# Four Strassen blocks per FFN, one more weight sum made by transfers, and sums ahead of splits

## The chip, the cores and the metric

The kernel runs on one core of one Trainium2 chip. The metric is device time in microseconds; three runs of the kernel before gave 925.48, 925.88 and 926.36, median 925.88.

## What is computed

A trunk of two encoder layers on 256 tokens of width 1024, all in float32. Each layer is FFN, mixer, FFN, each closed by a residual and a layer norm; the mixer is a bidirectional mLSTM in layer 0 and windowed attention in layer 1. The change touches the four FFNs alone:

```
def swiglu(x, w_in, w_out):                  # x: (256, 1024)
    gu = x @ w_in                            # w_in: (1024, 5632)
    g, u = gu[..., :D_FF], gu[..., D_FF:]    # D_FF = 2816
    return (jax.nn.silu(g) * u) @ w_out      # w_out: (2816, 1024)

x = layer_norm(ALPHA * x + 0.5 * swiglu(x, ...), g, b)
```

## The kernel before

**Split products.** A float32 matrix product is made of three TensorE matmuls: each operand is split into a high part (`_hi`, rounded to the matmul's type) and a low part (`_lo`, the remainder), and `mm3` adds hi·hi, hi·lo and lo·hi in PSUM. Activations are split once. Every weight piece, 128 partitions by 1024 values (512 KB), is loaded into a raw buffer, ScalarE (ACT) writes `w_hi` (`Weights.high`, L214) and VectorE (DVE) writes `w_lo` as raw minus hi (`Weights.low`, L238).

**An FFN before.** The 2816 gate columns and the same number of up columns are worked off as: 512 columns wide, plain; then three groups (`GROUPS`), each a 256-column unit (plain: 48 matmuls of 512 columns, weight pieces that hold 256 gate beside 256 up columns) and a 512-column block in Strassen's form (`seven`): the two token tiles, the two halves of the 1024 rows, and gate beside up make a 2x2 by 2x2 block product that takes seven products of 12 matmuls instead of eight. Between them stand the `w_out` chunks (`down`, 12 matmuls each into four banks `py`): 16 of an FFN's 22 chunks are spread over groups and blocks, the last six make the tail.

**The block.** Its weights are eight raw pieces in four quarters (two pieces each): b11, b12 and b22, held in the `s_raw` buffers, and the fourth one "a", loaded plainly through `w_raw`. Sums of quarters are made in place: b11 is split (s1), then DVE adds b12 to it, it is split again (s5), DVE adds b22, it is split again (s6), and the fourth quarter is added to it by an accumulating DMA that GpSimd (POOL) issues (L267). After s6 DVE also adds b22 to b12. Then b12, b22 and b11 are split. So a block has 14 splits, 6 sums on DVE and 2 accumulating DMAs; TensorE's seven products use the parts in the same order, and the sums of the activations (`S1` to `S4`) are made once per FFN. DVE and ACT also combine the products (tiles `e1`, `e2`, `e5`, `g1`), and TensorE turns the result for `w_out` (`tr`): token tile 0 at the block's end, token tile 1 in the next stretch of work; ACT and DVE write its `h_hi` and `h_lo`.

**What orders the work.** Splits and sums are recorded by a planner in the program, not by a hand-written order. `Paced` keeps a rough clock for each engine; after every TensorE instruction `Weights.fill` (L270) records further highs, lows and sums as long as ACT's and DVE's planned clocks are no more than 300 ns ahead of TensorE's, the raw data are due, and at most `RING` = 10 split pieces stand ahead of the ones in use. Within `fill` a low goes before a sum. What is recorded is a fixed order on each engine, and each engine works its order off one by one. Loads are issued by SyncE (SP) right after the low or sum that frees a buffer: four `w_raw` buffers, two more (`v_raw`) for the FFN's own pieces, and six `s_raw` buffers used in turn.

**The tail.** After the last block the planner is off: `take_rows(6)` (L884) records the splits of the last six chunks as far as they are still missing, `W.done(0)` records as many of the next stage's first splits as the ring has room for (four), and only then `tail` (L569) records the last products: six chunks for token tile 0 (two halves `o` of the columns), `norm[0].half` and the rest of its layer norm on DVE, and the same for token tile 1, with the turn of the last block's token tile 1 (`between`) after ten of token tile 0's twelve chunk products, and `emit_x` (the normalized tile is turned into `xT` for the next stage) near the end.

Of the kernel before, what the change touches and what calls it, by code (L numbers as in the profile page):

```python
# [16 lines left out]
D = 1024  # L17
# [6 lines left out]
GROUPS = 3  # L24
RAW_BUFS = 4
S_RAW = 6
# [120 lines left out]
class Weights:  # L147
# [5 lines left out]
    def __init__(self, nc, pool, words, plan, after):  # L153
        self.nc, self.pool, self.words, self.plan, self.after = nc, pool, words, plan, after
        self.raw, self.parts, self.half, self.sums = {}, {}, [], []
        self.made = self.used = self.room = 0
        self.todo = {tag: [i for i, w in enumerate(words) if w["tag"] == tag] for tag in ("w_raw", "s_raw")}
        self.free = {"w_raw": RAW_BUFS, "v_raw": 0, "s_raw": 0}
# [14 lines left out]

    def open(self, pool, end, s_raw=S_RAW, v_raw=V_RAW):

        self.spool, self.send, self.vbufs = pool, end, v_raw
        self.free["s_raw"], self.free["v_raw"] = s_raw, v_raw
        self.load()

    def load(self, most=None):  # L180
# [3 lines left out]
        while most is None or n < most:  # L184
# [10 lines left out]
            pool, bufs = {"w_raw": (self.pool, RAW_BUFS), "v_raw": (self.spool, self.vbufs), "s_raw": (self.spool, S_RAW)}[in_]  # L195
# [74 lines left out]
    def fill(self):  # L270

        nc = self.nc
        while True:
# [7 lines left out]
            if vec < nc.pe + AHEAD:  # L281
                if self.half and nc.when(self.half[0][1]) < vec + SOON:
                    self.low()
                    continue
                if self.sums and nc.when(*(self.raw[w] for w in self.sums[0][1:] if isinstance(w, int))) < vec + SOON:
                    self.sum()
                    continue
            break

    def take(self, n):  # L290
        i = self.used
        self.used += n
        self.split(self.used)
        return [self.parts[j] for j in range(i, i + n)]
# [4 lines left out]
    def done(self, upto=None, most=None, high_only=False):  # L299
# [3 lines left out]
        for j in [j for j in self.parts if j < upto]:  # L303
            del self.parts[j]
        self.room = max(self.room, upto + RING)
# [15 lines left out]
def trunk_kernel(ctx: ExitStack, tc: tile.TileContext, x, ffn_w_in, ffn_w_out, ln_g, ln_b, ml_w_in, ml_gate_b,  # L321
# [17 lines left out]
    def split_of(w, scale=None, needs=None):  # L339

        plan.append(dict(word=w, k=words[w]["k"], scale=scale, needs=needs))
        return len(plan) - 1
# [97 lines left out]
    W = Weights(nc, wpool, words, plan, after)  # L440
# [173 lines left out]
    def ffn(l, i, n, pending, last):  # L614
        with ExitStack() as ph:
# [170 lines left out]
            def seven(full, unit_turn):  # L786
# [36 lines left out]
                unit_turn()  # L823
# [16 lines left out]
            turn = None  # L840
            for g in range(GROUPS):
                ps = [wbank(), wbank()]
                pieces = []
                for a in range(4):
                    pieces.extend(W.take(1))
                    for t in range(2):
                        for k in (2 * a, 2 * a + 1):
                            mm3(ps[t], pair(xT, A, k, tok(t)), pair(pieces[a], A, k % 2), k == 0, k == 7)
                    W.done()
                    if g == 0 and not start:  # L850
                        for n_, f_ in zip(XP[1:], (x_three, x_two, x_four)):
                            if a == n_:
                                f_()
                    if a == 1:
                        if g:
                            turn()
                        else:
                            for t in range(0 if start else 1, 2):
                                tr(hB0, t, hs[t])
                hh = []  # L860
                for t in range(2):
                    sg = temp("sg")[:, 0:256]
                    nc.scalar.activation(sg, ps[t][:, 0:256], AF.Silu)
                    hh.append(temp("hh")[:, 0:256])
                    nc.vector.tensor_mul(hh[t], sg, ps[t][:, 256:512])
                hp = h_room(2)
                chunks(hp, 2)
                down(1)

                def unit_turn(hp=hp, hh=hh):  # L870
                    p = wbank((128, 2, S))
                    for t in range(2):
                        for k in range(2):
                            nc.tensor.transpose(p[:, k, tok(t)], hh[t][:, k * 128:(k + 1) * 128], ident)
                    split_evac(hp, p)

                down(1)
# [557 lines left out]
```

## Time and profile before

| | |
|---|---|
| median of three runs | 925.88 us |
| span of the profiled execution | 924.3 us |
| around the span (median less span) | 1.6 us |
| busy: TensorE, DVE, ACT, POOL | 914.6, 785.0, 544.8, 107.0 us |
| mean granted TensorE clock | 0.998 |
| one group (256-column unit and block), on TensorE | 47.7 us |

How to read the views: in the chain and the timeline a line is start, duration, engine, what, and in brackets the idle time just before it and who ended it. In the windows a line is the stretch, its length, then busy time and instruction count of PE (TensorE), PEld (weight loads), DVE, ACT and POOL, the granted clock, the DMA engines' busy share and GB/s. In the groups a line is line, engine, operation, output<-inputs, shapes and count, then busy time and mean ns of one.

### The profile page before, as it was taken

What the parts mean: (1) busy time and instruction counts of PE and PEld (TensorE: products, weight loads), DVE (VectorE), ACT (ScalarE), POOL (GpSimd) and SP (SyncE); (2) the same over time, 40 slices, a digit from 0 to 9 for tenths busy, and PEclk for the clock granted to TensorE, in tenths of its full rate; (3) what the DMA queues carried; (4) which work ended last, traced back from release to release, by engine and by line L of the source; (5) the groups of instructions that cost most, each with busy time, mean ns of one, the idle gap of its engine ahead of it and who ended that gap; (6) DMA issues with size and microseconds to landing.
All of it is one profiled execution on the core that took longest, in us unless ns stands there. A gap on an engine that the chain in (4) does not pass through costs nothing.

```text
span 924.3 us, 12533 instructions
## 1 busy us (share of the span) xinstructions
PE 914.6 (99%) x4507; PEld 767.0 (83%) x4507; DVE 785.0 (85%) x949; ACT 544.8 (59%) x765; POOL 107.0 (12%) x154
## 2 busy tenths in 40 slices
PE   9999999999999999999999999999999999999996
PEld 7788888889988888888888888888888888888885
DVE  5899997886799799988887898988869878998876
ACT  5656756446664548565636566565569555757460
POOL 0010103013211010101010101010435300110100
PEclk9999999999999999999999999999999999999999
DMA  8969773655635949685558697737434385969431
GB/s 276 361 166 333 203 277 73 227 160 177 212 103 171 343 117 341 169 305 137 160 172 328 151 327 210 262 76 228 148 127 137 94 272 204 276 194 343 124 88 45
DMA packets 98525, 187.55 MB, mean 203 GB/s; under 512 B 6776, under 2 KB 37520, under 8 KB 98464
## 3 DMA queue, kind: packets, MB, share of 16 engines
q1 hardware_dynamic: 91072, 173.04, 54.9%
q0 software_dynamic: 6816, 12.67, 8.6%
q10 hardware_dynamic: 576, 1.05, 0.3%
q8 instruction: 35, 0.57, 0.2%
q14 instruction: 26, 0.21, 0.1%
HBM read 185.68 MB, written 1.05 MB: 202 GB/s over the span
## 4 chain that ended last, share of the span: by engine, by line
PE 93%; DVE 3%; ACT 1%; DMA 1%; issue 1%; POOL 0%; SPq 0%; DVEq 0%; POOLq 0%; ACTq 0%
PE pw L138 60%; PE py L138 33%; DVE w_lo L138 1%; ACT w_hi L138 1%; DVE h L138 1%; DMA w_raw<-in_ffn_w_out_dram 1%; DMA w_raw<-in_ffn_w_in_dram 0%; POOL hrs L1072 0%; DVE wt L138 0%; DVE x L138 0%; DVE hst L138 0%; SPq L102 0%; ACT xT_hi L138 0%; DVE stats L138 0%; ACT sg L138 0%
## 5 line engine op out<-in xcount | busy, mean ns | idle before, releaser
L138 DVE TENSOR_TENSOR w_lo<-w_raw,w_hi 128x1024 fp32r<-128x1024 f32 (+1 forms) x237 | 281.6, 1219 | 24.7 <-ACT w_hi L138 21.6
L138 ACT CAST w_hi<-w_raw 128x1024 fp32r<-128x1024 f32 (+1 forms) x237 | 241.2, 1049 | 82.1 <-PE py L138 27.3
L138 PE MATMUL pw<-w_hi,xT_hi 128*128 128x512 f32 x560 | 221.6, 397 | 0.0
L138 PE MATMUL pw<-w_lo,xT_hi 128*128 128x512 f32 x560 | 217.6, 390 | 0.5 <-DVE w_lo L138 0.5
L138 PE MATMUL pw<-w_hi,xT_lo 128*128 128x512 f32 x560 | 218.0, 391 | 0.0
L138 ACT CAST w_hi<-s_raw 128x1024 fp32r<-128x1024 f32 x144 | 148.1, 1052 | 78.5 <-DVE s_raw L138 42.1
L138 DVE TENSOR_TENSOR w_lo<-s_raw,w_hi 128x1024 fp32r<-128x1024 f32 x144 | 172.9, 1220 | 21.6 <-ACT w_hi L138 21.0
L138 PE MATMUL py<-w_hi,h_hi 128*128 128x512 f32 x349 | 136.9, 392 | 0.0
L138 PE MATMUL py<-w_hi,h_lo 128*128 128x512 f32 x349 | 136.0, 390 | 0.0
L138 PE MATMUL py<-w_lo,h_hi 128*128 128x512 f32 x349 | 135.9, 390 | 0.0
L138 PEld LDWEIGHTS pw<-w_hi,xT_lo 128*128 128x128 f32 x560 | 105.0, 188 | 22.5
L138 PEld LDWEIGHTS pw<-w_lo,xT_hi 128*128 128x128 f32 x560 | 105.3, 188 | 22.0 <-DVE w_lo L138 1.6
L138 PEld LDWEIGHTS pw<-w_hi,xT_hi 128*128 128x128 f32 x560 | 105.1, 188 | 20.0
L267 POOL DMA_DIRECT2D s_raw<-in_ffn_w_in_dram x24 | 29.2, 1217 | 511.6 <-DVE w_lo L138 429.0
L138 DVE TENSOR_TENSOR s_raw<-s_raw 128x1024 f32<-128x1024 f32 x72 | 87.2, 1221 | 1.0
L138 PEld LDWEIGHTS py<-w_hi,h_lo 128*128 128x128 f32 x349 | 65.5, 188 | 13.8
L138 PEld LDWEIGHTS py<-w_lo,h_hi 128*128 128x128 f32 x349 | 65.6, 188 | 13.6 <-DVE w_lo L138 0.3
L138 PEld LDWEIGHTS py<-w_hi,h_hi 128*128 128x128 f32 x349 | 65.5, 188 | 13.2
L138 PE MATMUL pw<-w_hi,S_hi 128*128 128x512 f32 x192 | 74.7, 389 | 0.0
L138 PE MATMUL pw<-w_lo,S_hi 128*128 128x512 f32 x192 | 74.7, 389 | 0.0
L138 PE MATMUL pw<-w_hi,S_lo 128*128 128x512 f32 x192 | 74.7, 389 | 0.0
L138 DVE TENSOR_TENSOR h_lo<-pw,h_hi 128x512 fp32r<-128x512 f32 x44 | 30.2, 688 | 26.5 <-ACT h_hi L138 26.5
(205 smaller groups left out, 1102.3 us busy)
## 6 DMA issues: line engine op xcount, KB each, us to landing
w_raw<-in_ffn_w_out_dram SPq DMA_DIRECT2D x88, 512.0 KB, 5.3
s_raw<-in_ffn_w_in_dram SPq DMA_DIRECT2D x72, 512.0 KB, 6.0
w_raw<-in_ffn_w_in_dram SPq DMA_DIRECT2D x56, 512.0 KB, 4.8
w_raw<-in_ffn_w_in_dram SPq DMA_DIRECT2D x96, 256.0 KB, 3.9
s_raw<-in_ffn_w_in_dram POOLq DMA_DIRECT2D x24, 512.0 KB, 6.0
w_raw<-in_ml_w_in_dram SPq DMA_DIRECT2D x24, 512.0 KB, 4.7
w_raw<-in_at_w_in_dram SPq DMA_DIRECT2D x12, 512.0 KB, 4.9
w_raw<-in_ml_w_out_dram SPq DMA_DIRECT2D x8, 512.0 KB, 4.1
```

The costliest lines, as they stand in the source:

```text
L138: r = f(out, *args, **kw)
L267: nc.gpsimd.dma_start(t.rearrange("p (k f) -> p k f", k=self.words[w]["k"]), v, accum_op=OP.add)
```

## The change

- Three groups become one 256-column unit (with its two `down` chunks) and four blocks in a row, each with four `down` chunks but the last, which has two. The unit's loop body is now straight code.
- In a block one more sum goes to DMA: after s1 and its DVE sum, an accumulating DMA adds to b12 the same weights that b22 holds (rows 512 and up of the up columns, read once more from memory), instead of DVE adding b22 to it after s6. A block then has 14 splits, 4 sums on DVE and 4 accumulating DMAs.
- `fill` now records a due sum before a low.
- The order of splits and the order of use part: chunks `down(1)` and `down(3)` are split ahead of the pieces that wait for sums, and used after them (`turn` += 2.5); the ring counts from the oldest piece not yet used.
- The six `s_raw` buffers become three tags of two (`s_raw0` to `s_raw2`), rotated from block to block so that the next b11 takes the buffers of the b12 before it.
- The layer norm's gain and bias rows take the tag `s_raw1`.

```
-GROUPS = 3
+SEVENS = 4
-S_RAW = 6
+S_RAW = 2
+TAGS = ("w_raw", "s_raw0", "s_raw1", "s_raw2")
...
             if vec < nc.pe + AHEAD:
+                if self.sums and nc.when(*(self.raw[w] for w in self.sums[0][1:] if isinstance(w, int))) < vec + SOON:
+                    self.sum()
+                    continue
                 if self.half and nc.when(self.half[0][1]) < vec + SOON:
                     self.low()
                     continue
-                if self.sums and nc.when(*(self.raw[w] for w in self.sums[0][1:] if isinstance(w, int))) < vec + SOON:
-                    self.sum()
-                    continue
...
     def take(self, n):
-        i = self.used
+        these = self.order[self.used:self.used + n]
         self.used += n
-        self.split(self.used)
-        return [self.parts[j] for j in range(i, i + n)]
+        self.split(max(these) + 1)
+        return [self.parts[j] for j in these]
...
-        self.room = max(self.room, upto + RING)
+        while self.gone < upto:
+            j = self.order[self.gone]
+            self.left.discard(j)
+            self.parts.pop(j, None)
+            self.gone += 1
+        self.room = max(self.room, min(self.left, default=len(self.plan)) + RING)
...
-    def seven(w, c0, c1, downs):
+    def seven(w, c0, c1, n, downs):
...
-        b12, b11, b22 = ([word(x, 2, "s_raw") for x in at(*p)] for p in ((0, c1), (0, c0), (512, c1)))
+        b12, b11, b22 = ([word(x, 2, TAGS[1 + (r + n) % 3]) for x in at(*p)]
+                         for r, p in ((1, (0, c1)), (0, (0, c0)), (2, (512, c1))))
         s1 = [split_of(w_) for w_ in b11]
         for a in at(512, c0):
             piece(a, 2)
-        for j in range(2):
-            after[s1[j]] = [(b11[j], b12[j])]
+        for j, a in enumerate(at(512, c1)):
+            after[s1[j]] = [(b11[j], b12[j]), (b12[j], a)]
         downs(0)
         s5 = [split_of(w_, None, p) for w_, p in zip(b11, s1)]
+        downs(1)
         for j in range(2):
             after[s5[j]] = [(b11[j], b22[j])]
         s6 = [split_of(w_, None, p) for w_, p in zip(b11, s5)]
         for j, a in enumerate(at(512, c0)):
-            after[s6[j]] = [(b11[j], a), (b12[j], b22[j])]
-        downs(1)
-        [split_of(w_, None, p) for w_, p in zip(b12, s6)]
+            after[s6[j]] = [(b11[j], a)]
+        plan[s6[0] - 1]["turn"] += 2.5
+        [split_of(w_, None, p) for w_, p in zip(b12, s1)]
         for w_ in b22:
             split_of(w_)
         downs(2)
+        downs(3)
         [split_of(w_, None, p) for w_, p in zip(b11, s6)]
-        downs(3)
+        if n < SEVENS - 1:
+            plan[-3]["turn"] += 2.5
...
-            for g in range(GROUPS):
-                c0 = 512 + 768 * g
-                for a in range(4):
-                    beside(wi, a * 256, c0, F + c0)
-                down(2)
-                seven(wi, c0 + 256, F + c0 + 256, lambda i_: down(1) if g < GROUPS - 1 or i_ < 2 else None)
+            for a in range(4):
+                beside(wi, a * 256, 512, F + 512)
+            down(2)
+            for g in range(SEVENS):
+                c0 = 768 + 512 * g
+                seven(wi, c0, F + c0, g, lambda i_: down(1) if g < SEVENS - 1 or i_ < 2 else None)
             down(6)
...
-            gb = load_ln(lambda name: pool.tile([128, D], F32, name=name, tag="s_raw", bufs=S_RAW), l, n)
+            gb = load_ln(lambda name: pool.tile([128, D], F32, name=name, tag=TAGS[1 + SEVENS % 3], bufs=S_RAW), l, n)
```

More of the change, by code (lines that the diff above doesn't have):

```diff
@@ L784, in copied, with seven @@
                 return e
-            def seven(full, unit_turn):
+            def seven(full, before):
                 of = lambda k0, t: (lambda k: pair(xT, A, k0 + k, tok(t)))
@@ L838, in seven @@
                 return lambda: tr(hB, 1, v["u1"])
[L840 to L860, printed above, removed]
-                for t in range(2):
[L862 to L877, printed above, removed]
-                turn = seven(g < GROUPS - 1, unit_turn)
-                if start and g == GROUPS - 1:
-                    small_loads()
@@ new lines, in ffn @@
+            ps = [wbank(), wbank()]
+            pieces = []
+            for a in range(4):
+                pieces.extend(W.take(1))
+                for t in range(2):
+                    for k in (2 * a, 2 * a + 1):
+                        mm3(ps[t], pair(xT, A, k, tok(t)), pair(pieces[a], A, k % 2), k == 0, k == 7)
+                W.done()
+                if not start:
+                    for n_, f_ in zip(XP[1:], (x_three, x_two, x_four)):
+                        if a == n_:
+                            f_()
+                if a == 1:
+                    for t in range(0 if start else 1, 2):
+                        tr(hB0, t, hs[t])
@@ new lines, in ffn, with turn @@
+            hh = []
+            for t in range(2):
+                sg = temp("sg")[:, 0:256]
+                nc.scalar.activation(sg, ps[t][:, 0:256], AF.Silu)
+                hh.append(temp("hh")[:, 0:256])
+                nc.vector.tensor_mul(hh[t], sg, ps[t][:, 256:512])
+            hp = h_room(2)
+            chunks(hp, 2)
+            down(1)
+            def turn():
+                p = wbank((128, 2, S))
+                for t in range(2):
+                    for k in range(2):
+                        nc.tensor.transpose(p[:, k, tok(t)], hh[t][:, k * 128:(k + 1) * 128], ident)
+                split_evac(hp, p)
```

29 lines of the change are left out of this document (18 added, 11 removed).

## The prediction

> **What bounds the kernel now.** I read the page's head and chain first, then the chain in order of time (start, duration, what), the window of one group (its length, then busy time of PE, PEld, DVE, ACT, POOL, granted clock, DMA share, GB/s), and last the timeline of each engine around an FFN's tail.
>
> ```profile
> span 924.3 us, 12533 instructions
> PE 914.6 (99%) x4507; PEld 767.0 (83%) x4507; DVE 785.0 (85%) x949; ACT 544.8 (59%) x765; POOL 107.0 (12%) x154
> PE 93%; DVE 3%; ACT 1%; DMA 1%; issue 1%; POOL 0%; SPq 0%; DVEq 0%; POOLq 0%; ACTq 0%
> ...
> 62.74 2.97 PE py L138 x12
> ...
> 377.15 5.44 PE py L138 x24
> 382.59 5.93 PE pw L138 x28
> ...
> 365.80:413.50 47.70, 47.70 (x218) 39.49 (x217) 44.32 (x44) 30.82 (x36) 2.39 (x2) 1.00 0.80 257
> ```
>
> TensorE is busy for 99% of the span and is 93% of the chain that ends last. 24 matmuls take 5.44 us: one each 0.2267 us (a record lasts longer, since they overlap); 28 with four transposes take 5.93, so four transposes cost 0.49. A group (204 matmuls, 12 transposes) is 46.2 + 1.5 = 47.7 us, just what its window is: TensorE never waits in it, with DVE busy for 44.3 of it. So matmuls saved are time saved, as long as DVE, DMA and the order of work keep up.
>
> **Part 1: fewer matmuls.** Two 256-column units (48 matmuls each) go, one block (84) comes: 12 fewer per FFN, 48 in all; in the built order the PE instructions fall from 4509 to 4461, transposes unchanged. 48 x 0.2267 = **-10.9 us**, all on the path.
>
> **Part 2: DVE's and ACT's work.** The built order has 24 more splits, 8 fewer DVE sums and more small products' work.
>
> ```profile
> L138 DVE TENSOR_TENSOR w_lo<-s_raw,w_hi 128x1024 fp32r<-128x1024 f32 x144 | 172.9, 1220 | 21.6 <-ACT w_hi L138 21.0
> ...
> 454.14 2.35 DVE L138 TENSOR_TENSOR w_lo<-w_raw,w_hi 128x1024 fp32r<-128x1024 f32 x2
> 456.41 0.68 DVE L138 TENSOR_TENSOR h_lo<-pw,h_hi 128x512 fp32r<-128x512 f32 x1
> 457.01 0.68 DVE L138 TENSOR_TENSOR e<-g,e 128x512 f32<-128x512 f32 x1
> 457.61 2.51 DVE L138 TENSOR_TENSOR w_lo<-w_raw,w_hi 128x1024 fp32r<-128x1024 f32 x2
> ```
>
> One low lasts 1.22, two end after 2.35, so the pitch is 1.14; for 128x512 it is 0.60 (456.41 to 457.01). A block with four `down` chunks takes TensorE 132 x 0.2267 + 8 transposes (0.98) = 30.9 us. DVE's part was 24 x 1.14 + 7 x 0.60 = 31.6 and becomes 22 x 1.14 + 4.2 = 29.3. Before, a block ran over by 0.7 and the unit behind it gave that back; now blocks follow each other with 1.6 us to spare each, and the last one (TensorE 25.5, two chunks fewer; DVE 27.0) runs over by 1.5. I cost the blocks at nothing: the cover is this 1.6 plus the lead of the splits. The built order shows that lead, counted in TensorE time from an evacuation to the first use of the next piece not yet split: some 9 to 21 us in the blocks of before from the second on, now 4 to 13 in every block. In the first block of an FFN it was already down to 7.0 before (5.7 and 2.95 in the first FFN), and the only wait there is the 2.97 at 62.74, 0.25 over 12 x 0.2267. In that place the lead is now 7.5: **-0.25**.
>
> **Part 3: transfers.** Rows of the DMA issues and queues, of two windows, and of one issue by itself:
>
> ```profile
> s_raw<-in_ffn_w_in_dram POOLq DMA_DIRECT2D x24, 512.0 KB, 6.0
> q0 software_dynamic: 6816, 12.67, 8.6%
> 386.00:388.00 2.00, 2.00 (x10) 1.60 (x10) 1.27 (x2) 2.00 (x3) 0.00 (x0) 1.00 1.13 197
> 396.00:398.00 2.00, 2.00 (x11) 1.65 (x10) 1.93 (x2) 1.71 (x4) 0.00 (x0) 1.00 1.05 392
> s_raw<-in_ffn_w_in_dram POOLq DMA_DIRECT2D x1, 512.0 KB, 7.5
> ```
>
> 24 accumulating transfers become 64. While two of them run (386 to 388) the DMA engines move 197 GB/s, without them 392; their share of the span, 8.6% of 924.3 over 24, is 3.3 us each, against 0.524/0.392 = 1.34 for a load. A block then needs 12 x 1.34 + 4 x 3.3 = 29.3 of its 30.9 us: 95%. The urgent ones are the two into b11. By the built order the second is issued behind the second s6 low, 7.8 us into the block (6.0 where DVE takes the second product, + 0.6 + 1.14), and b11's low stands ahead of DVE's reading of the fifth product, which ends at 19.5 (seven stretches of 2.72 and four transposes); less 1.05 for the high and 1.22 for the low, 9.5 us may pass. The trace has 6.0 as the median and 7.5 as the slowest (the last row, the second of a pair). So nothing is charged, with little room. By the Trainium skill, "DMA: Bandwidth & Descriptors", "Anatomy of one DMA — SWDGE (gpsimd) path", a transfer issued from GpSimd takes about 2 us plus its bytes at 436 GB/s, an estimate of 3.2 us, and the room would be twice as large; the row's 6.0 decides. POOL's 40 added issues wait for DVE, but nothing that others need soon is queued behind them.
>
> **Part 4: the tail gives it back.** Here I read the built order of after against the timeline of before: DVE and one line of ACT, then PE.
>
> ```profile
> 450.54 2.36 DVE L138 TENSOR_TENSOR w_lo<-w_raw,w_hi 128x1024 fp32r<-128x1024 f32 x2
> 457.81 1.05 ACT L138 CAST w_hi<-w_raw 128x1024 fp32r<-128x1024 f32 x1 [0.52 <-DMA w_raw<-in_ffn_w_in_dram]
> 460.04 0.68 DVE L138 SCALAR_TENSOR_TENSOR x<-x,py 128x512 f32<-128x512 f32 x1
> 460.75 0.69 DVE L138 BATCH_NORM_STATS2 stats<-x 128x6 f32<-128x512 f32 x1
> 463.65 0.69 DVE L138 TENSOR_TENSOR h_lo<-pw,h_hi 128x512 fp32r<-128x512 f32 x1 [2.20 <-ACT h_hi L138]
> 464.42 0.69 DVE L138 SCALAR_TENSOR_TENSOR x<-x,py 128x512 f32<-128x512 f32 x1
> 467.91 1.28 DVE L138 SCALAR_TENSOR_TENSOR x<-x,rs,ln_b 128x1024 f32<-128x1024 f32 x1 [0.46 <-POOL rs L553]
> 469.12 2.36 DVE L138 TENSOR_TENSOR w_lo<-w_raw,w_hi 128x1024 fp32r<-128x1024 f32 x2
> 471.38 0.68 DVE L138 SCALAR_TENSOR_TENSOR x<-x,py 128x512 f32<-128x512 f32 x1
> 472.71 1.27 DVE L138 TENSOR_TENSOR xT_lo<-py,xT_hi 128x512 fp32r<-128x512 f32 x2
> 455.74 0.40 PE L138 MATMUL py<-w_lo,h_hi 128*128 128x512 f32 x1
> 466.03 0.39 PE L138 MATMUL py<-w_hi,h_lo 128*128 128x512 f32 x1
> 471.02 1.03 PE L138 MATMUL py<-ident,x 128*128 128x128 f32 x8
> 473.73 0.39 PE L138 MATMUL pw<-w_hi,xT_lo 128*128 128x512 f32 x1
> ```
>
> All times here are those of the second FFN before. The tail's first low part is used at 455.74, one more chunk every 0.68; all six had been split before. In the built order of after only four stand ahead of `e<-g,e` (457.01; it needs the last product, so it can't move up). Chunks five and six come behind it: ready at 458.83 and 459.97, needed at 458.48 and 459.16. TensorE is 0.4 late, then 0.85 in all.
>
> Behind them four lows of the next stage stand ahead of `x<-x,py` (two before). The last two read pieces whose loads are issued only once the lows of chunks five and six free their buffers. Before, the second low of 450.54 ended at 452.90, and ACT waited until 457.81 for the piece that took its buffer: 4.9 us. So the last piece lands at 464.9, its high ends at 465.9, its low starts there and lets `x<-x,py` start at 467.1; the statistics follow 0.7 later, `h_lo` 0.6 after that, done at 469.1. On ACT the `h_hi` of the same turn is also queued behind the two highs that wait for loads. TensorE wants this `h_lo` at 466.03, 0.85 later by now: it waits 2.2 more, **3.1 in all**. In the first FFN three chunks are late by 2.0 together, and `h_lo` then costs 1.1: 3.1 again. The third is like the second.
>
> The layer norm ends on time: its last step starts 3.5 behind the second `x<-x,py` (464.42 to 467.91), so at 472.7, done at 474.0; the turn of x is due at 471.02 + 3.1. But `xT_lo` starts 4.8 after that last step with two lows between (467.91 to 472.71), so at 477.5, first half done at 478.1; wanted at 473.73 + 3.1 = 476.8: **1.3** more in the second FFN, and with one low fewer between them **0.2** in the first and the third. The last FFN has no next stage: **0.85**. Sum of the tails: 3 x 3.1 + 1.3 + 0.4 + 0.85 = **+11.9**.
>
> **The sum.** 924.3 - 10.9 - 0.25 + 11.9 = 925.0, and with the 1.6 between the span and the median of 925.88: **926.6 us**. What a measurement of this kernel can tell from no change is about 0.2%, or 1.85 us: 924.0 to 927.7 count as the same. The uncertain size is the 4.9; two rows of the DMA issues bound it, and a window serves a rival below.
>
> ```profile
> w_raw<-in_at_w_out_dram SPq DMA_DIRECT2D x8, 512.0 KB, 3.5
> s_raw<-in_ffn_w_in_dram SPq DMA_DIRECT2D x72, 512.0 KB, 6.0
> 900.30:924.30 24.00, 16.97 (x86) 14.19 (x84) 14.32 (x26) 1.28 (x3) 1.85 (x2) 0.94 0.12 44
> ```
>
> With a landing of 3.5, the shortest median, the waits for `h_lo` shrink by 1.4, 1.4 and 1.1: 922.7. With 6.0, the longest, each of the three grows by 1.1: 929.9. That is the likeliest case's own range. I take 4.9 as it was paid in the same place by the same kind of pair.
>
> **The rivals.**
>
> *Most of the gain stays.* The next stage's pieces land before the late chunks are through, so `h_lo` isn't late and only late chunks cost (2.0 + 3 x 0.85 = 4.55): 924.3 - 10.9 - 0.25 + 4.55 + 1.6 = 919.3. For it: 99% busy and a clean 10.9. Against it: 2.2 of 4.9 us would have to go from the landing, and the shortest row has 3.5.
>
> *The accumulating transfers set the pace: slower.* In each block b11's highs wait for them on ACT, DVE's lows behind that, and behind those the reading of the products that frees TensorE's banks. It decides from a landing of 9.5 us on; each 0.5 beyond costs that in 16 blocks: 8 us, 934.6. For it: 95% of the DMA engines' time, and loads of the next block's b11 and b12 start while they run. Against it: 7.5 at most so far, in the same company of loads.
>
> *TensorE's clock falls after the tails' waits.* The only stretch with a lowered clock, 0.94, is the last 24 us, where TensorE idles for 7. If 2.2 us of waiting did the same to a tail of 18 us (455.74 to 473.73), each of three would cost 1.1: 929.9. Against it: every other stretch that I looked at has 1.00. By the Trainium skill, "TensorE: Matmul & The Clock Gate", "Part 1: The HAM clock gate", the clock halves after an idle window of about 3.4 us, which 2.2 stays under, and an estimate for one such fall is 1.7 us; no stretch here shows it.
>
> That fewer matmuls are run is settled by the built order.
>
> **The numbers.** Tail as worked out 56%, most of the gain stays 15%, transfers set the pace 24%, clock 5%. Within the first, 6 points are below 924.0 and 15 above 927.7. So faster 0.21, same 0.35, slower 0.44. The range must leave out no more than a tenth on each side: 919.3 is kept as its low end, and above, the transfer case up to 0.65 us a block (10.4): 937.
>
> **What would show it.** PE's span of a full block at 30.9 us and no wait in it; between `e<-g,e` and the first `x<-x,py` of an FFN's tail six to seven lows instead of two or three, the last two behind an ACT wait for DMA; a TensorE wait of about 2 us for `h_lo` in three tails. It is wrong if the tails stay at 18 us, if full blocks take over 31 us, or if accumulating transfers land after more than 9.5.

## The result: 968.4 us, slower by 4.6%

Four runs of the changed kernel gave 965.64 to 971.71 us, median 968.36; the kernel before had 925.74 beside them. The ratio is 1.046, with a 95% interval of 1.044 to 1.0485. The forecast was 926.6, with 937 as the high end of its range. The profiled execution has a span of 966.3 us, 42.0 more than before. First the head of its page, with the chain, one DMA queue and the two landings that count:

```profile
span 966.3 us, 12569 instructions
PE 921.5 (95%) x4459; PEld 764.5 (79%) x4459; DVE 810.0 (84%) x969; ACT 568.3 (59%) x793; POOL 155.2 (16%) x194
...
q0 software_dynamic: 17696, 33.65, 20.6%
PE 43%; DVE 19%; DMA 15%; issue 15%; ACT 4%; POOL 3%; SPq 0%; DVEq 0%; POOLq 0%; ACTq 0%
...
s_raw<-in_ffn_w_in_dram SPq DMA_DIRECT2D x96, 512.0 KB, 8.6
...
s_raw<-in_ffn_w_in_dram POOLq DMA_DIRECT2D x64, 512.0 KB, 6.8
```

TensorE has 48 matmuls fewer, as foreseen, but it is down from 99% to 95% of the span, and only 43% of the chain that ends last is still its own. The rest goes through DVE, the DMA and "issue". What TensorE waited for (total, times, longest):

```profile
PE pw L139 <- DVE e L139: 20.6, 10, 3.0
PE py L139 <- DVE h_lo L139: 6.2, 4, 2.0
PE py L139 <- ACT h_hi L139: 3.4, 2, 1.7
PE py L139 <- DVE w_lo L139: 2.7, 10, 0.9
PE pw L139 <- ACT w_hi L139: 1.7, 1, 1.7
```

The second to fifth rows are nearly all from the tails, the six chunks and the layer norm behind an FFN's last block. The first is new: ten waits inside blocks, at the turn of the finished half block (`tr`). A wait ends a run of overlapped matmuls, so each also costs some 0.16 us that the records don't show as idle (a record lasts 0.39, the pitch is 0.2267). Over the whole span TensorE's waits grew from 2.7 to 37.8 us, their hidden part is about 4, and 27.3 us at half clock cost another 13.7. Less the 10.9 of the matmuls that is about 42, the difference of the spans.

Four blocks one by one, each from its first product to the next block's first, in the windows (length, then busy time and count of PE, PEld, DVE, ACT, POOL, granted clock, DMA share, GB/s): the first of the first FFN, the second and third of the second FFN, the third of the third.

```profile
48.54:82.42 33.88, 31.04 (x141) 25.48 (x140) 30.09 (x31) 21.52 (x27) 5.50 (x5) 1.00 0.93 255
382.30:413.18 30.88, 30.88 (x142) 25.56 (x141) 28.78 (x29) 21.25 (x25) 4.81 (x4) 1.00 0.94 261
413.18:450.01 36.83, 33.85 (x142) 27.63 (x141) 30.58 (x31) 21.35 (x25) 4.87 (x4) 0.91 0.88 247
599.79:635.28 35.49, 32.70 (x142) 26.66 (x141) 30.41 (x31) 21.23 (x25) 4.85 (x4) 0.95 0.89 246
```

The second row is the block of the prediction: 30.88 us, TensorE never idle, DMA engines at 94%. So the block can run at that pace. But of twelve distances between blocks only three are 30.88; the others reach 36.8, and together they are 29.1 us too long. The lines of one late block, in order of time, POOL's, ACT's, DVE's and PE's from the timeline:

```profile
59.49 2.44 POOL L272 DMA_DIRECT2D s_raw<-in_ffn_w_in_dram  x2 [10.30 <-DVE w_lo L139]
71.56 2.95 ACT L139 CAST w_hi<-s_raw 128x1024 fp32r<-128x1024 f32 x3 [5.21 <-DMA s_raw<-in_ffn_w_in_dram]
72.65 2.36 DVE L139 TENSOR_TENSOR w_lo<-s_raw,w_hi 128x1024 fp32r<-128x1024 f32 x2 [3.72 <-ACT w_hi L139]
74.93 0.69 DVE L139 TENSOR_TENSOR e<-pw,e 128x512 f32<-128x512 f32 x1
75.65 0.69 DVE L139 TENSOR_TENSOR e<-e,e 128x512 f32<-128x512 f32 x1
76.49 0.63 PE L139 MATMUL pw<-ident,e 128*128 128x128 f32 x4 [2.84 <-DVE e L139]
```

The two late transfers into b11 are issued back to back from 59.49 on. ACT stands 5.21 us for the second, its high comes at 71.56, DVE has two lows to do, then reads the product, multiplies, and only then may TensorE turn the half block, 2.84 us late. How long the transfers took shows in the DMA issues of short windows around single issues (the last number is the time to landing): the first and the second of this pair, then the second of the pair in the clean block at 382.30.

```profile
s_raw<-in_ffn_w_in_dram POOLq DMA_DIRECT2D x1, 512.0 KB, 5.7
...
s_raw<-in_ffn_w_in_dram POOLq DMA_DIRECT2D x1, 512.0 KB, 10.9
...
s_raw<-in_ffn_w_in_dram POOLq DMA_DIRECT2D x1, 512.0 KB, 8.5
```

10.9 in the late block, 8.5 in the clean one; the prediction put the limit at 9.5, for a transfer issued 7.8 us into the block.

### The profile page after: what moved, and what is told of

The parts are those of the page before. It is cut to its first block, busy times and chain, and to the rows that moved or that the text cites. A ratio compares the mean times of both kernels' runs of the same rounds, so it can differ in the third digit from the quotient of the medians.

```text
span 966.3 us, 12569 instructions
## 1 busy us (share of the span) xinstructions
PE 921.5 (95%) x4459; PEld 764.5 (79%) x4459; DVE 810.0 (84%) x969; ACT 568.3 (59%) x793; POOL 155.2 (16%) x194
## 4 chain that ended last, share of the span: by engine, by line
PE 43%; DVE 19%; DMA 15%; issue 15%; ACT 4%; POOL 3%; SPq 0%; DVEq 0%; POOLq 0%; ACTq 0%
PE pw L139 28%; PE py L139 15%; DMA s_raw<-in_ffn_w_in_dram 11%; DVE w_lo L139 9%; ACT w_hi L139 3%; DVE s_raw L139 3%; DVE e L139 2%; POOL s_raw L272 2%; DMA w_raw<-in_ffn_w_out_dram 1%; DMA w_raw<-in_ml_w_in_dram 1%; DMA w_raw<-in_ffn_w_in_dram 1%; DVE h_lo L139 1%; DMA w_raw<-in_at_w_in_dram 1%; DVE x L139 1%; DVE h L139 1%
## 5 line engine op out<-in xcount | busy, mean ns | idle before, releaser
L139 DVE TENSOR_TENSOR w_lo<-w_raw,w_hi 128x1024 fp32r<-128x1024 f32 (+1 forms) x213 | 253.8, 1219 | 28.9 <-ACT w_hi L139 26.8
L139 DVE TENSOR_TENSOR w_lo<-s_raw,w_hi 128x1024 fp32r<-128x1024 f32 x192 | 227.5, 1219 | 52.1 <-ACT w_hi L139 47.8
L139 ACT CAST w_hi<-w_raw 128x1024 fp32r<-128x1024 f32 (+1 forms) x213 | 216.1, 1046 | 69.4 <-PE py L139 22.1
L139 ACT CAST w_hi<-s_raw 128x1024 fp32r<-128x1024 f32 x192 | 191.9, 1051 | 79.4 <-DMA s_raw<-in_ffn_w_in_dram 50.0
L139 PE MATMUL pw<-w_hi,xT_hi 128*128 128x512 f32 x480 | 193.5, 404 | 1.7 <-ACT w_hi L139 1.7
L139 PE MATMUL pw<-w_hi,xT_lo 128*128 128x512 f32 x480 | 189.1, 395 | 0.8 <-DVE xT_lo L139 0.8
L139 PE MATMUL pw<-w_lo,xT_hi 128*128 128x512 f32 x480 | 188.9, 395 | 0.4 <-DVE w_lo L139 0.4
L272 POOL DMA_DIRECT2D s_raw<-in_ffn_w_in_dram x64 | 77.7, 1232 | 519.4 <-ACT w_hi L139 158.5
L139 PEld LDWEIGHTS pw<-w_hi,xT_hi 128*128 128x128 f32 x480 | 91.6, 191 | 19.6 <-ACT w_hi L139 2.1
L139 PEld LDWEIGHTS py<-w_hi,h_hi 128*128 128x128 f32 x349 | 66.7, 191 | 17.8 <-ACT h_hi L139 4.3
L139 DVE TENSOR_TENSOR s_raw<-s_raw,s_raw 128x1024 f32<-128x1024 f32 x64 | 78.3, 1224 | 2.5 <-DMA s_raw<-in_ffn_w_in_dram 0.8
L139 ACT COPY e<-pw 128x512 f32<-128x512 f32 x48 | 28.2, 587 | 61.7 <-PE pw L139 61.7
```

Source lines behind the costliest of these rows:

```text
L139: r = f(out, *args, **kw)
L272: nc.gpsimd.dma_start(t.rearrange("p (k f) -> p k f", k=self.words[w]["k"]), v, accum_op=OP.add)
```

## The experiments

Every run took place beside the kernel before (925.8 to 926.3). "Blocks" is what the twelve distances between the first `S_hi` matmuls of an FFN's blocks have over 12 x 30.88 us; "rest" is everything else (tails, other stages, last blocks), counted from the same of e2, whose span is 913.2. All in us, from the profiled execution; "half" is the time at half clock. e2, e5 and e11 leave out a sum that one of a block's seven products needs, so they show where time goes and are no replacement; the other runs compute the same as the kernel before.

| run | median | ratio to before, 95% | blocks | rest | half |
|---|---|---|---|---|---|
| changed kernel | 968.4 | 1.044 to 1.0485 | 29.1 | 25.0 | 33.4 |
| e1 planned landing 11.5 | 993.3 | 1.071 to 1.074 | 25.8 | 52.1 | 38.8 |
| e2 no late transfers | 915.1 | 0.987 to 0.990 | 0.9 | 0.0 | 3.9 |
| e3 b12 on DVE | 961.9 | 1.037 to 1.040 | 6.1 | 42.7 | 15.5 |
| e4 next stage held | 986.7 | 1.063 to 1.069 | 29.7 | 41.7 | 36.5 |
| e5 late transfers plain | 935.9 | 1.009 to 1.012 | 0.0 | 21.5 | 11.6 |
| e6 chunk behind s6 | 964.9 | 1.0405 to 1.044 | 21.9 | 30.5 | 28.8 |
| e7 two chunks ahead | 968.2 | 1.041 to 1.047 | 34.7 | 19.6 | 32.6 |
| e8 before, b12 by transfer | 953.5 | 1.0275 to 1.0315 | | | 17.2 |
| e9 b11 on DVE | 945.7 | 1.020 to 1.023 | 6.0 | 26.7 | 19.6 |
| e10 one sum of b11 each way | 936.8 | 1.0105 to 1.0135 | 0.0 | 23.6 | 21.7 |
| e11 as e5, planned 4.5 | 920.0 | 0.992 to 0.996 | 1.6 | 3.3 | 5.2 |
| e12 lows before sums | 963.5 | 1.039 to 1.042 | 18.5 | 29.4 | 22.1 |
| e13 as e10, planned 5.5 | 929.0 | 1.002 to 1.004 | 7.3 | 7.3 | 9.8 |
| e14 as e13, chunks ahead | 938.8 | 1.0115 to 1.014 | 9.6 | 16.0 | 16.2 |
| e15 changed, planned 5.5 | 952.4 | 1.025 to 1.0285 | 31.6 | 7.1 | 24.3 |
| e16 before, planned 5.5 | 925.8 | 0.9986 to 1.0005 | | | |
| e17 as e10, last block 4.5 | 925.8 | 0.998 to 1.000 | 0.0 | 12.8 | 8.9 |

Against the ranges named before each run: e3 (theory Q's), e7, e9, e11, e12, e15, e16 and e17 fell into one of theirs; e2 and e10 came out better than any; e5, e6 and e13 between their two; e1, e4, e8 and e14 worse than any.

**e1: plan for a later landing.**

```
-ADDING = 8000.0
+ADDING = 11500.0
```

> The planner's figure for the landing of an accumulating transfer goes from 8.0 to 11.5 us; the transfers stay as many. Theory Q (queue order): the second transfer into b11 lands up to 10.6 us after its issue, the low of that piece stands on DVE ahead of the reading of the fifth product, and TensorE waits behind that. With 11.5 the low is planned behind the reading, so the ten waits for e (20.6 us, and 0.16 each that the record hides) go, and with them the 17.1 us at half clock inside blocks (8.5): 968 becomes 935 to 942, every full block but an FFN's first is 30.9. Theory B (bandwidth): 16 pairs more of transfers of 3.1 us each fill the DMA engines, so the block can't be shorter than they allow: the wait moves from e to the low of b11 or of the next block, blocks stay at 33 to 36, 960 to 970.

All waits for `e` are gone and seven of twelve blocks have 30.88 us (one of them 30.90), so the queue order did make that wait. But the splits of one list are made in one order: a b11 low put later puts every split behind it later, and TensorE now waits 36.2 us for `w_lo` at products and 9.1 at chunks. Order alone is not the cause; theory B's picture (the wait moves) is what happened, worse than it said.

**e2: without the late transfers.**

```
-            after[s6[j]] = [(b11[j], a)]
+            after[s6[j]] = []
```

> The second accumulating transfer of each pair of pieces, the one into b11 after the sixth product's split (32 of 64), is left out, so one of a block's seven products uses a wrong sum. Theories Q and B both say that ACT's 50 us of waits for s_raw and TensorE's 20.6 for e go: 935 to 942, blocks of 30.9. If the waits for e stay, neither is right and DVE is what is late.

```profile
span 913.2 us, 12491 instructions
...
PE 903.3 (99%) x4459; PEld 758.2 (83%) x4459; DVE 808.9 (89%) x969; ACT 573.1 (63%) x793; POOL 116.1 (13%) x162
```

Far better than expected: 913.2 is the prediction's 924.3 less 10.9 and 0.25 to the tenth, with b12's transfers, DVE's work, the new order and the tails' code as in the changed kernel. Eleven of twelve blocks are 30.88 (the other 31.73, with a wait of 0.7 for `e`), and TensorE waits nowhere in the tails. So all 53 us that the changed kernel has more than this hang on the late sum into b11, in the blocks and in the tails.

**e3: the new sum back on DVE.**

```
-            after[s1[j]] = [(b11[j], b12[j]), (b12[j], a)]
+            after[s1[j]] = [(b11[j], b12[j])]
...
-            after[s6[j]] = [(b11[j], a)]
+            after[s6[j]] = [(b11[j], a), (b12[j], b22[j])]
...
-        [split_of(w_, None, p) for w_, p in zip(b12, s1)]
+        [split_of(w_, None, p) for w_, p in zip(b12, s6)]
```

> The new sum goes back to DVE and to its old place (b22 into b12 after the sixth split), four blocks and the rest stay: 32 accumulating transfers instead of 64, two DVE sums of 1.14 more in each block (31.6 of 30.9 us). Theory B: with 74% instead of 95% of the DMA engines' time the transfers land after 6 to 7.5 us, the waits for e go and DVE's 0.7 a block is left: 940 to 948. Theory Q: the transfers into b11 are issued and land as late as before (the second about 1.24 behind the first and served after it), the waits stay within a third: 955 to 975.

The waits for `e` went (0.16 left) and the blocks fell from 29.1 over to 6.1, as B says; the time lies in Q's range. B against Q is not decided, for the edit also moved the pair apart: a DVE sum now stands between the two lows, the second transfer is issued 2.3 to 2.6 us behind the first (1.9 once) where it was mostly 1.1, and lands after 6.0 to 8.1. The rest grew by 17.7, which neither theory had. DVE has 31.6 us of work for a block's 30.9 and falls behind: a pair's first transfer is issued 7.4 us into the second FFN's first block and 13.7 into its last.

**e4: hold the next stage back in the tails.**

```
-            W.done(0)
+            W.done(0, 0)
```

> No new high of the next stage is planned between an FFN's last chunk and its tail, so three lows of the next stage fewer stand ahead of the first x<-x,py. By the prediction's fourth part the waits for h_lo and h_hi in the first three tails (1.73+1.96, 1.95, 1.68+1.96 = 9.3 us) go and with them the 10.2 us at half clock there (5.1): 968 becomes 952 to 956. If only order moves and the pieces land late anyway, the wait turns up again at xT_lo or at the next stage's first pieces: 962 to 968.

The waits for `h_hi` and `h_lo` went, as the prediction's fourth part says, and came back larger at the next stage's first pieces (2.43, 0.48, 0.23, 0.76, 1.67 and 0.76 us behind the first FFN alone). A cure of the symptom: those splits are late, wherever they are put.

**e5: the late transfers without adding.**

```
-            nc.gpsimd.dma_start(t.rearrange("p (k f) -> p k f", k=self.words[w]["k"]), v, accum_op=OP.add)
+            r = t.rearrange("p (k f) -> p k f", k=self.words[w]["k"])
+            if isinstance(v, tuple):
+                nc.gpsimd.dma_start(r, v[0])
+            else:
+                nc.gpsimd.dma_start(r, v, accum_op=OP.add)
...
-            after[s6[j]] = [(b11[j], a)]
+            after[s6[j]] = [(b11[j], (a,))]
```

The tuple marks the transfers into b11.

> The 32 late transfers into b11 stay in their place, on their queue and behind the same lows, but write without adding, so one of a block's seven products uses a wrong sum. Leaving them out altogether gave 915.1. Theory A (the adding is slow: 3.1 us of the DMA engines each and one after the other, second of a pair landing after 10 us): a plain one takes 1.3 us of the engines, the pair lands after 4 to 6, the waits for e and most of the tails go: 915 to 928. Theory D (the dependence alone: low, transfer, high, low, then everything behind it in the planned order): 940 to 965, with blocks of 32 to 35 left.

The same places, lows and queue, and all twelve blocks run at 30.88. The second of a pair lands after 4.8 to 7.6 us. So the blocks' 29 us come from these transfers adding, which makes them land later and holds the DMA engines longer, and not from the dependence as such. The tails keep 21.5, so these are another matter.

**e6 and e7: other places in the order.** The first edit is e6's, the second e7's.

```
-        downs(1)
         for j in range(2):
             after[s5[j]] = [(b11[j], b22[j])]
...
-        plan[s6[0] - 1]["turn"] += 2.5
+        downs(1)
```

```
         if n < SEVENS - 1:
             plan[-3]["turn"] += 2.5
+        else:
+            plan[-3]["turn"] += 2.6
+            plan[-4]["turn"] += 3.5
...
-                seven(wi, c0, F + c0, g, lambda i_: down(1) if g < SEVENS - 1 or i_ < 2 else None)
-            down(6)
+                seven(wi, c0, F + c0, g, lambda i_: down(1))
+            down(4)
```

> The small chunk that is split between the fifth and the sixth product's weights is split behind the sixth's, so on DVE one low fewer (1.14 us) stands ahead of the transfers into b11. Theory A or D, with the time of issue as the lever: the waits for e shrink by 1.1 or more in each of the ten places, one or two halvings of the clock go: 945 to 962. If DVE is simply busy all the time and the bubble that the chunk filled now opens, 966 to 975.

> In the last block of each FFN two of the six last chunks are split ahead of b11 (used behind it, as before). The tails cost 24 us more than in the run without the late transfers. Theory T (the chunks are late because they are planned behind b11's late transfer): the waits for w_lo, h_hi and h_lo in the tails shrink to a third: 950 to 960. If the next stage's last pieces are what is late, whatever stands ahead of them: 963 to 970.

e6 came near its expectation in the blocks (7.2 us less) and lost most of it in the tails (5.5 more). e7 misses theory T: the chunks' waits went, the rest fell by 5.4 and the blocks grew by 5.6. Moving one step about doesn't help while b11 is late.

**e8: the transfer alone, in the kernel before.**

```
-        for j in range(2):
-            after[s1[j]] = [(b11[j], b12[j])]
+        for j, a in enumerate(at(512, c1)):
+            after[s1[j]] = [(b11[j], b12[j]), (b12[j], a)]
...
-            after[s6[j]] = [(b11[j], a), (b12[j], b22[j])]
+            after[s6[j]] = [(b11[j], a)]
...
-        [split_of(w_, None, p) for w_, p in zip(b12, s6)]
+        [split_of(w_, None, p) for w_, p in zip(b12, s1)]
```

> The kernel before with one edit: b22 is added to b12 by an accumulating transfer behind the first sum (48 such transfers instead of 24), three groups with their 256-column units as they were. Theory P (the period decides: 30.9 us leave no room for a chain that 47.7 us hides): 923 to 928. Theory N (the number of transfers decides, they slow down b11's): waits for e or w_lo in the groups, 932 to 945.

```profile
PE py L138 <- DVE w_lo L138: 6.5, 13, 1.6
PE pw L138 <- DVE w_lo L138: 6.3, 6, 1.2
PE py L138 <- DVE h_lo L138: 3.9, 2, 2.0
```

It cost 27 us, more than either theory had. Of this only 1.2 us stand in the last distance between groups of each of three FFNs; the rest is behind it, in the last blocks and the tails (chunks, `h_hi`, `h_lo`, and 12 us more at half clock). One edit of the change is thus harmful by itself, with three groups too. Two things came with it: more transfers, and more pieces that the planner takes to be due only 8 us after their issue. This run can't tell them apart.

**e9 and e10: b11's late sums by DVE, both or the second.**

```
-        for a in at(512, c0):
-            piece(a, 2)
+        aw = [word(a, 2) for a in at(512, c0)]
+        [split_of(w_) for w_ in aw]
...
-            after[s6[j]] = [(b11[j], a)]
+            after[s6[j]] = [(b11[j], aw[j])]              # e9
+            after[s6[j]] = [(b11[j], (a, aw[j])[j])]      # e10
```

> The late sum into b11 is done by DVE from the piece that was loaded for the second product (held until then), the new sum into b12 stays a transfer: 32 accumulating transfers, DVE 31.6 us of a block's 30.9 (as in the run with b12 on DVE, which took 961.9, with its blocks at 30.9 to 31.7 but its tails 43 us longer than without the late transfers). Theory W (which of the sums goes by transfer decides: b12's is issued early and nobody waits, b11's is waited for): no ACT wait for s_raw, blocks of 30.9 to 32, and 935 to 950. Theory N (the number of transfers decides, whichever): about the same as with b12 on DVE, 955 to 965.

> Of the two late sums into b11 the second goes to DVE, the first stays a transfer: 48 accumulating transfers, none queued behind another in a pair, DVE 30.4 of 30.9 us. Theory A (the second of the pair, served after the first and landing 9 to 10.6 us after its issue, is what is late): waits for e down to a quarter, 940 to 952. If a lone transfer at 5.4 us is late too: 955 to 970.

e9 against e3: the same number of transfers and of DVE sums, the same blocks (6.0 and 6.1), but 16 us less in the rest. So which sum goes by transfer matters, as W says, and the time lies in W's range; in the blocks alone it made no difference. e10 is the sharpest of all: one transfer of the pair less, and every one of the twelve distances is 30.88, with correct sums. A window of the length of one such block and the landing of the lone transfer in it:

```profile
579.71:610.59 30.88, 30.88 (x141) 25.56 (x140) 30.68 (x31) 21.32 (x26) 3.61 (x3) 1.00 0.84 253
...
s_raw<-in_ffn_w_in_dram POOLq DMA_DIRECT2D x1, 512.0 KB, 6.0
```

DVE is busy for 30.68 of 30.88 us and nothing waits: the prediction's second part, that DVE can be filled to the brim, holds. Shown, then: with the second transfer of the pair left to DVE, or with both there but not adding (e5), the blocks are on time.

**e11, e13, e15, e16: the planner's figure.** The edit is `ADDING = 4500.0` on e5 (e11), and `ADDING = 5500.0` on e10 (e13), on the changed kernel (e15) and on the kernel before (e16).

> The late transfers into b11 without adding (one product of seven with a wrong sum, 935.9 us, blocks clean, tails 20.6 us longer than without them) and the planner's figure for a transfer's landing at 4.5 us instead of 8.0, so that in the built order all six last chunks are split ahead of e<-g,e again in three of the four FFNs. Theory T (the tails cost what the planner's late place for b11's last split makes them cost, not what the transfer takes): 915 to 921. If the chunks and the next stage's pieces land late whatever is planned: 930 to 938.

> One late sum into b11 by DVE and one by a transfer (936.8 us with blocks of 30.88), and the planner's figure for a transfer's landing at 5.5 us instead of 8.0, which is what the lone transfers took there (5.0 to 5.6). In the built order five to three lows instead of seven to six stand between e<-g,e and the first x<-x,py of the tails. Theory T: the tails' waits for chunks, h_hi and h_lo shrink to a third or less, blocks stay 30.88: 918 to 926. If the tails' cost is in the landing of the next stage's pieces and not in the planned order: 933 to 938.

> The changed kernel with nothing but the planner's figure at 5.5 us; its pairs of transfers stay, the second landing after 7.5 to 10.6. Theory A+T: the tails get shorter by 10 to 18 us, the blocks' waits for e stay or grow, since the late low is planned still earlier: 948 to 965. If the planner's figure alone was the trouble: 915 to 930.

> The kernel before with the planner's figure at 5.5 us: 924 to 929, since its tails have all six chunks split ahead already and its transfers into b11 have a unit's time to land. Below 922 would mean that the gain of the two kernels above comes from this figure and not from the four blocks.

In all three kernels with four blocks the rest falls to a third or less, from 21.5 to 3.3, from 23.6 to 7.3 and from 25.0 to 7.1, though e13's lone transfers still land after 5.7 to 6.0 us and e15's second ones after up to 11.3. The splits of the last six chunks stand behind b11's in the list; a b11 planned as due 8 us after its issue puts them, and the next stage's splits behind them, behind `e<-g,e`. The price is in the blocks: in e13 ten short waits for `e` (4.9 us in all), in e15 25.7 us of them. The kernel before gains nothing from the figure.

**e12: lows before sums again** (the two `if`s in `fill` swapped back).

> The planner looks at lows ahead of sums again, as it did before the change. A sum later by a low or two delays b11's chain (sum, high, low, transfer) by 1.1 to 2.3 us a step: 968 to 980 if the order of the chain matters; the same within 0.5% (963 to 973) if the planner's choice seldom differs.

Slightly faster than the changed kernel, 963.5, at the edge of the second range: the part of the change that put sums ahead of lows is worth nothing or a little less.

**e14 and e17: towards a kernel with both causes gone.** e14 is e13 with the edit of e7. e17 is e10 with a planned landing of 4.5 for the last block's b11 alone:

```
-            nc.mark(t, max(nc.vec, nc.pe) + ADDING)
+            nc.mark(t, max(nc.vec, nc.pe) + self.words[w].get("adding", ADDING))
...
+        if n == SEVENS - 1:
+            words[b11[0]]["adding"] = 4500.0
```

> As the last, and two of the six last chunks are split ahead of the last block's b11. The built order then has three, one, one and no lows in that place. Theory T: 915 to 921, near the 915.1 of the run without the late transfers. If two chunks ahead of b11 only push b11's low late (as with the transfers in pairs, where this edit gave nothing): 925 to 935.

> As the run with one late sum by DVE and one by a transfer (936.8 us: every block 30.88, tails 20.6 us), with the planner's figure at 4.5 us for the last block of each FFN alone, 8.0 elsewhere. With 5.5 everywhere the tails came down to about 8 us, but each block grew by 0.6, because the late low was planned ahead of the reading of the fifth product (929.0). Theory: here blocks stay 30.88 as in the first and tails are about 8 us as in the second: 915.1 + 8 = 920 to 925, below the kernel before. If the blocks' plan carries over into the tails (four lows instead of three stand in that place in the second and third FFN): 925 to 930.

e14 lost again, mostly at the next stage's pieces. e17 kept all blocks at 30.88 and brought the rest from 23.6 to 12.8, not to 8: 925.8 against 926.3, a ratio of 0.9992 with an interval of 0.998 to 1.000. That is the best version with four blocks and correct sums, 4.4% under the changed kernel and no better than the kernel before by more than can be measured. What it lacks to e2's 915.1 lies behind the twelve distances, in the last blocks and the tails.

## Why the prediction was wrong

**Part 1 held**: e2's span of 913.2 is 924.3 - 10.9 - 0.25. That this fits to the tenth is partly luck: the 0.25 doesn't show by itself, e2's first block is 0.85 longer than the others, and it has 1.1 us less of half clock at its end than the kernel before. **Part 2 held**: but for that one block, none of the twelve in e2, e5 or e10 is longer than 30.9, and in e10 DVE is 99% busy.

**Part 3 is the step that failed.** It charged nothing for the transfers, and the blocks alone cost 29.1 us. It had the second transfer into b11 issued 7.8 us into the block and landed within 7.5, so 15.3 in, with 17.3 as the limit (7.8 + 9.5). In the changed kernel (KB of loads counted from the packets that start while the transfer is under way):

| blocks | second issued, us into the block | landed, us after issue | landed, us into the block | loads beside it, KB | wait for `e`, us |
|---|---|---|---|---|---|
| three clean ones | 9.3 | 8.3 to 8.5 | 17.7 to 17.8 | 720 to 752 | none |
| first of the second and third FFN | 8.7, 8.8 | 8.5, 8.7 | 17.3, 17.4 | 766, 844 | 0.96, 0.31 |
| the other seven | 9.4 to 12.1 | 10.2 to 11.1 | 19.6 to 22.9 | 1260 to 1362 | 2.3 to 3.0 |
| last block of the first three FFNs | 9.6 to 10.6 | 7.4 to 7.5 | 17.0 to 18.0 | 0 to 4 | none |

The limit was near: at 17.3 to 17.8 us in, blocks are clean or wait for less than 1 us, and beyond 19.5 all wait. Both sizes that were held against it were wrong, and both signs that the prediction named for this came: full blocks over 31 us, and landings beyond 9.5.

```profile
389.51 0.68 DVE L139 TENSOR_TENSOR e<-e,pw 128x512 f32<-128x512 f32 x1
390.11 3.49 DVE L139 TENSOR_TENSOR w_lo<-s_raw,w_hi 128x1024 fp32r<-128x1024 f32 x3
391.63 1.20 POOL L272 DMA_DIRECT2D s_raw<-in_ffn_w_in_dram  x1 [0.29 <-DVE w_lo L139]
...
420.28 0.68 DVE L139 TENSOR_TENSOR e<-e,pw 128x512 f32<-128x512 f32 x1
420.88 4.62 DVE L139 TENSOR_TENSOR w_lo<-s_raw,w_hi 128x1024 fp32r<-128x1024 f32 x4
422.78 2.47 POOL L272 DMA_DIRECT2D s_raw<-in_ffn_w_in_dram  x2 [11.80 <-DVE w_lo L139]
```

The issue is late: DVE takes the second product (`e<-e,pw`) 7.2 us into the clean block that begins at 382.30, not 6.0, with one low behind it before the second transfer; in the late block from 413.18 two lows stand there, and the second transfer goes out at 423.5. In the late block from 48.54 it goes out at 60.6. Lateness of issue alone did no harm: in e5 the second transfers are issued 8.7 to 12.3 us in, and all twelve blocks are clean.

The landing is late too. The prediction read it from the kernel before, where the two of a pair are issued 2.3 to 3.5 us apart and a transfer has at most 601 KB of loads beside it: 7.5 at most there, 10.2 to 11.1 here, where the pair mostly goes out 1.1 us apart and the next block's four loads follow 0.9 behind it. The median of 6.0 and the slowest of 7.5 were not bounds but samples of a queue at a lower load, and the prediction itself had put that load at 95%.

The rival that the transfers set the pace had a chance of 24% and is what happened in the blocks, but its price, 0.5 us a block and 934.6 in all, was too low: seven late blocks cost a wait of 2.3 to 3.0 each, and four of these another 1.7 to 3.4 of half clock.

**Part 4 had the mechanism and half the size.** The tail as foreseen, in the first FFN (ACT, DVE, then PE):

```profile
187.41 1.05 ACT L139 CAST w_hi<-w_raw 128x1024 fp32r<-128x1024 f32 x1 [3.90 <-DMA w_raw<-in_ml_w_in_dram]
188.49 2.58 DVE L139 TENSOR_TENSOR w_lo<-w_raw,w_hi 128x1024 fp32r<-128x1024 f32 x2 [3.73 <-ACT w_hi L139]
190.99 0.68 DVE L139 SCALAR_TENSOR_TENSOR x<-x,py 128x512 f32<-128x512 f32 x1
190.35 0.50 PE L139 MATMUL py<-w_hi,h_hi 128*128 128x512 f32 x1 [1.73 <-ACT h_hi L139]
193.04 0.80 PE L139 MATMUL py<-w_hi,h_lo 128*128 128x512 f32 x1 [1.96 <-DVE h_lo L139]
```

ACT stands for the next stage's piece, DVE's last lows and `x<-x,py` come behind it, and TensorE waits for `h_lo`: about 2 us in three tails were forecast, 1.95 to 1.96 were measured. Not priced were the wait for `h_hi` just before (1.73 and 1.68 in two tails) and the half clock behind the two (10.2 us long, so 5.1). With clean blocks (e5, e10) the rest cost 21.5 to 23.6, and in the changed kernel 25.0, where +11.9 was forecast; what it hung on, the planned place of b11's last split, the prediction had seen in the built order but taken as given.

**The clock** was a rival of 5% at three places of 1.1. There were six half-clock stretches besides the one at the end, 13.7 us, and most of that in blocks.

## What to carry to other kernels

A landing time read at one load is no bound at another: when a change nearly triples the transfers of one queue, cost the second of a pair as served after the first, and take the time of issue from the engine's real lead, not from its count of instructions. In a list that is worked off in one order, a piece that is due late delays everything planned behind it, so half of the harm may turn up in a tail that the piece has nothing to do with; the run that leaves the piece out shows this at once. And where a bound sits at the edge, ask what a wait costs beyond itself: here the clock added a third to the waits.

## What the hardware showed that was not expected

**A wait halves the clock by where it falls on a fixed grid.** All half-clock stretches of a run begin on one grid of 3.413 us, whose phase differs from run to run. Windows of the changed kernel on that grid (PE's busy time is the second number, the granted clock the third from the end):

```profile
75.16:78.57 3.41, 2.08 (x11) 1.81 (x12) 3.38 (x5) 2.66 (x4) 0.55 (x1) 1.00 1.02 384
140.01:143.42 3.41, 1.10 (x6) 0.63 (x5) 3.38 (x5) 3.27 (x4) 0.00 (x0) 1.00 1.04 416
143.42:146.84 3.42, 3.42 (x11) 2.83 (x12) 3.42 (x4) 1.53 (x2) 1.20 (x1) 0.50 0.67 244
836.33:839.74 3.41, 1.49 (x7) 0.91 (x5) 3.38 (x5) 1.82 (x2) 1.19 (x1) 1.00 1.01 363
```

The wait of 2.84 us that ended at 76.49 was cut in two by the grid and cost no clock; the one of 2.31 that ended at 143.36 lay within one window and halved the next. Over the full-clock windows of all 19 traces of this case, each of the 72 with TensorE busy for less than 1.47 us was followed by half clock, and none of those with more than 1.71; between the two it went either way (the window of the last row was followed by full clock). One wait of 1.96 us can be enough, as here in e17:

```profile
177.57:180.98 3.41, 1.43 (x6) 0.57 (x5) 3.35 (x5) 0.48 (x1) 0.00 (x0) 1.00 0.84 299
180.98:184.40 3.42, 3.42 (x9) 2.64 (x9) 2.84 (x6) 1.04 (x1) 1.54 (x1) 0.50 0.22 84
```

The Trainium skill, "TensorE: Matmul & The Clock Gate", section "Part 1: The HAM clock gate", has a free-running window of 3413 ns, and the trace agrees; it speaks of an idle window, and there the measurement decides: 57% idle was enough, so the 2.2 us that the prediction thought safe are not, when they fall into one window.

**Two adding transfers 1.1 us apart run one after the other.** In the packets of the changed kernel's first late pair the first transfer moves its data from 1.9 to 5.4 us after its issue, and the second's begin 5.5 us after its own, 6.6 after the first's. The Trainium skill, "DMA: Bandwidth & Descriptors", section "SWDGE vs HWDGE vs iDMA", says that only one such queue is allocated, which fits. By the fit of the same page, section "Anatomy of one DMA — SWDGE (gpsimd) path", 2 us and the bytes at 436 GB/s, a transfer would take 3.2 us, an estimate far below the 5.7 and 10.9 of this pair. How late the second lands goes with the loads beside it, as the table above has it: 7.4 to 7.5 us with none, in last blocks with the same 1.1 us between the issues, 8.3 to 8.7 with 720 to 844 KB, 10.2 to 11.1 with 1260 to 1362. One pair stands outside this: in the last block of the last FFN it was 11.4 with 1024 KB. A transfer that takes longer also meets more loads, and no run changed these loads alone, so this is not shown to be the cause.
